# Heads' gated outputs go through device memory, and the first branch product becomes one stage over 16 row tiles behind the second branch's

## The chip, the cores and the metric

The kernel runs on one core of one Trainium2 chip. The metric is the device time of one launch in microseconds (us): lower is better. The kernel before takes 1253.05 us, the median of three runs (1251.77 to 1256.2).

## The reference

One layer of a hybrid decoder for a prompt group of 512 tokens and a sample group of 8 sequences of 4 tokens, 544 tokens in all, each of width 1024. Cut to what matters:

```
z = rmsnorm(h) @ W_in            # columns: q | k | v | gate | u | gv | gA | gB
q, k = rotary(q), rotary(k) / 16
o, s_new = retention(q, k, v, s0)        # 4 heads, decay per head; sample group starts from state s0
y_a = silu(gate) * rmsnorm_per_head(o)   # 4 heads x 512 = 2048 wide
gv  = layernorm(gelu(gv))
y_b = gelu(u) * spatial_gating(gv)       # 1024 wide
h += (sigmoid(gA) * (y_a @ W_br_a) + sigmoid(gB) * (y_b @ W_br_b)) @ W_o
h += relu(rmsnorm(h) @ W_up)**2 @ W_down # 4096 wide
h += sigmoid(rmsnorm(h) @ W_pg) * (p @ W_pp)
y = rmsnorm(h)
```

Outputs are y for both groups, the retention states of both groups, and the sample group's gv. All arithmetic counts as float32.

## The kernel before

Activations lie feature by token: a "slot" is a tile of 128 features by 544 tokens (`[P, T]`), and 56 slots, later 68 and 74, are handed out in turn by `get` and `put` (the slot freed longest ago comes first). A float32 operand is split into a high part (rounded, by a copy on ScalarE, line 127) and a low part (a subtraction on VectorE, line 128). TensorE takes three products for each: high times high, high times low, low times high.

A weight slab is 128 by 1024 values (512 KB). `Feed` loads slabs in the order in which they were planned (lines 535 to 573) into `raw` buffers, splits them ahead of use into "wide" buffers `hl`, and hands them to the products by `take`. There are four `hl` buffers (`ROOM1`), in the whole program. A "plain" product (`tile_of`, `dense`, line 315) makes one tile of 128 features: 8 steps over k, each of 3 products by 2 token halves of 272, so 48 matmuls. A "fast" run (`fast_run`, line 404) makes two tiles with 7 block products of 12 matmuls in place of 8, by sums of weight blocks and of activation blocks (Strassen's scheme with seven products). A pair takes three wide buffers, `w0`, `w1`, `w3`, and a small one. The copy on line 426 takes the first block product out of `fa` so that the next can add to it, and TensorE waits for that copy.

The stages in order:

- Four heads. Each makes two query and two key tiles, turns them (`rotary`, lines 685 to 690), makes four value tiles (`values`) and four gate tiles (`gates`). Around them stand the small steps of retention: transposes of the sample group's keys (`sample_keys`; GpSimd copies them out, line 787, TensorE transposes the copy, line 790), `scores` (line 849), the states' load, update and store (`state_ahead`, `sample_state`, 8 for each head, four buffers), `prompt_output`, and then `group_norm` and `group_normed`, which leave the head's four tiles of y_a as eight split slots `c.ya`.
- `branch_a(h, ya)`: for each of 8 output tiles, 4 steps over k, 24 matmuls. For heads 0 to 2 it is called in the next head, between its first pair of value tiles and the second. ScalarE copies each result from PSUM (line 711), and GpSimd issues an accumulating DMA to device memory, `acc_d` (line 712). For head 3 it stands alone behind the gv stage; there the eight sums are loaded again (line 702), and VectorE adds the products (line 715).
- gv: 4 fast pairs with transposes (`gated_by_token`); then branch_a for head 3, under which gv's layer norm is made; u: 4 fast pairs with `spatial`; gate A: 4 fast pairs, multiplied into the sums at once; gate B: 4 fast pairs, with the split of y_b (`gated`) beside them.
- y_b @ W_br_b tile by tile, with `merged` (lines 1216, 1217); W_o; the wide layer; the embedding gate; the last norm.

What sets the order: the small steps are put on a list with a due time (`chores`, `later`), and `tick` runs the due ones; a plain product ticks once every 12 matmuls, and a fast pair seven times. The due times are tables at the top (`QK`, `KEYS`, `SCORES`, `STATE`, `END`, `XOPS`). On top of that a scheduler places the instructions of each engine by its own estimate, and only pinned ones keep the program's order. Each engine then works strictly in that order.

Of the kernel before, what the change touches and what calls it, by code (L numbers as in the profile page):

```python
# [8 lines left out]
F32 = mybir.dt.float32  # L9
# [5 lines left out]
P = 128  # L15
# [8 lines left out]
H = 4  # L24
# [8 lines left out]
MORE = (12, 6)  # L33
ROOM1 = (4, 4, 1, 5)
ROOM2 = (1, 0, 0, 6)
# [3 lines left out]
STATES = 4  # L39
# [5 lines left out]
QK = ((7, 8, 9, 10), (0, 18, 2, 20))  # L45
KEYS = ((11, 16, 17), (22, 27, 28))
SCORES = (16, 24)
# [5 lines left out]
END = (17, 18, 22, 30)  # L53
# [37 lines left out]
def layer(tc, a, o):  # L91
    nc = tc.nc
    act, dve, pool, pe = nc.scalar, nc.vector, nc.gpsimd, nc.tensor
    with ExitStack() as ctx:
# [436 lines left out]
        def plan_branch_a(h):  # L531
            for m2 in range(4):
                feed.plan("plain", a["w_br_a"][4 * h + m2])

        for h in range(H):
            for p in range(6):
# [6 lines left out]
                if h and p == 2:  # L543
                    plan_branch_a(h - 1)
        for i in range(48, 56, 2):
            feed.plan("fast", a["w_in"][i], a["w_in"][i + 1])
        plan_branch_a(H - 1)
        for i in range(56, 80, 2):
            feed.plan("fast", a["w_in"][i], a["w_in"][i + 1])
        for n in ("w_br_b", "w_o"):  # L550
            for k in range(8):
                feed.plan("plain", a[n][k])
# [140 lines left out]
        acc_a = [None] * KD  # L693
        dp = enter(tc.tile_pool(name="sums", bufs=1, space=bass.MemoryType.DRAM))
        acc_d = [dp.tile([P, T], F32, tag=f"a{m}", name=f"acc{m}") for m in range(KD)]

        def branch_a(h, ya):

            if h == H - 1:
                for m in range(KD):  # L700
                    acc_a[m] = get()
                    nc.sync.dma_start(acc_a[m], acc_d[m])
            for m2 in range(4):
                w = feed.take()
                for i in range(2):
                    m = 2 * m2 + i
                    ps = Product()
                    dense(ps, [(*at(w, k * 256 + i * P), *ya[k]) for k in range(4)])
                    if h < H - 1:
                        t = get()  # L710
                        act.copy(halves(t), ps.all)
                        pool.dma_start(acc_d[m], t, accum_op=ALU.add if h else ALU.bypass)
# [3 lines left out]
            for y in ya:  # L716
                put(*y)
# [480 lines left out]
        for x in gvt:  # L1198
            put(*x)
# [372 lines left out]
```

## Time and profile before

| | |
|---|---|
| time, median of 3 runs (range) | 1253.05 us (1251.77 to 1256.2) |
| profiled execution, its own time | 1253.85 us |
| its span, first to last instruction | 1252.2 us |
| TensorE busy | 1226.6 us, 98% |
| VectorE, ScalarE, GpSimd busy | 900.4, 652.1, 101.9 us |
| granted TensorE clock, mean | 0.995 |
| DMA | 193.16 MB, mean 154 GB/s |

Line numbers are those of the kernel before. In a row of the chain or of the timeline, `f`, `fa`, `sc`, `ks` are PSUM tiles, `s` is any slot, `hl` a split weight slab, `acc` the sums in device memory, `x12` the number of instructions, and square brackets hold the idle time of the engine ahead of the row and what ended it. Matmul records can be missing, a few in a hundred, so a count of a little under the true number is no sign. The 1.65 us between the profiled execution's own time and its span lie around the program.

### The profile page before, as it was taken

What the parts mean: (1) busy time and instruction counts of PE and PEld (TensorE: products, weight loads), DVE (VectorE), ACT (ScalarE), POOL (GpSimd) and SP (SyncE); (2) the same over time, 40 slices, a digit from 0 to 9 for tenths busy, and PEclk for the clock granted to TensorE, in tenths of its full rate; (3) what the DMA queues carried; (4) which work ended last, traced back from release to release, by engine and by line L of the source; (5) the groups of instructions that cost most, each with busy time, mean ns of one, the idle gap of its engine ahead of it and who ended that gap; (6) DMA issues with size and microseconds to landing.
All of it is one profiled execution on the core that took longest, in us unless ns stands there. A gap on an engine that the chain in (4) does not pass through costs nothing.

```text
span 1252.2 us, 22976 instructions
## 1 busy us (share of the span) xinstructions
PE 1226.6 (98%) x9336; PEld 1196.7 (96%) x9336; DVE 900.4 (72%) x1341; ACT 652.1 (52%) x1106; POOL 101.9 (8%) x135
## 2 busy tenths in 40 slices
PE   8999999999999989999999999999999999999996
PEld 8998999999989988899999999999999999999996
DVE  6976957774767556678678645559449888878966
ACT  7553545444643555573466532436238558467733
POOL 0001111102010111111000000000000100000000
PEclk9999999999999999999999999999999999999999
DMA  8428544727664665675456462223346666766402
GB/s 284 168 93 272 168 157 134 245 100 168 170 223 133 164 157 175 220 203 142 119 138 178 146 211 94 85 85 99 105 101 179 175 178 160 182 165 180 140 1 72
DMA packets 73754, 193.16 MB, mean 154 GB/s; under 512 B 8400, under 2 KB 11728, under 8 KB 73648
## 3 DMA queue, kind: packets, MB, share of 16 engines
q1 hardware_dynamic: 58608, 141.42, 34.1%
q0 software_dynamic: 15040, 50.27, 18.0%
q8 instruction: 73, 1.20, 0.4%
q14 instruction: 33, 0.27, 0.1%
HBM read 163.74 MB, written 27.92 MB: 153 GB/s over the span
## 4 chain that ended last, share of the span: by engine, by line
PE 81%; DVE 5%; DMA 4%; issue 4%; ACT 3%; POOL 1%; SPq 0%; DVEq 0%; ACTq 0%; POOLq 0%
PE f L315 35%; PE fa L404 18%; PE f L404 14%; PE pg L315 4%; PE o L491 2%; PE st L491 2%; DMA acc<-s 1%; DVE hl L128 1%; PE so L914 1%; PE sc L491 1%; PE so L915 1%; ACT hl L127 1%; DVE s L128 1%; PE su L917 1%; DMA s<-in_xT 1%
## 5 line engine op out<-in xcount | busy, mean ns | idle before, releaser
L315 PE MATMUL f<-s,hl 128*128 128x272 f32 x4320 | 574.1, 290 | 3.4 <-ACT s L646 1.5
L315 PEld LDWEIGHTS f<-s,hl 128*128 128x128 f32 x4320 | 559.2, 189 | 11.5 <-ACT s L646 1.8
L128 DVE TENSOR_TENSOR hl<-raw,hl 128x1024 fp32r<-128x1024 f32 (+2 forms) x275 | 301.4, 1112 | 116.7 <-ACT hl L127 114.6
L127 ACT CAST hl<-raw 128x1024 fp32r<-128x1024 f32 (+2 forms) x275 | 259.9, 960 | 172.4 <-PE f L315 89.2
L404 PE MATMUL fa<-s,hl 128*128 128x272 f32 x2112 | 296.0, 289 | 3.9 <-ACT s L426 3.6
L404 PEld LDWEIGHTS fa<-s,hl 128*128 128x128 f32 x2112 | 276.0, 188 | 5.7 <-ACT s L426 4.6
L404 PE MATMUL f<-s,hl 128*128 128x272 f32 x1584 | 227.5, 290 | 1.4 <-ACT s L437 1.2
L404 PEld LDWEIGHTS f<-s,hl 128*128 128x128 f32 x1584 | 209.7, 189 | 2.8 <-ACT s L437 2.3
L127 ACT CAST s<-s 128x544 fp32r<-128x544 f32 (+4 forms) x170 | 97.4, 598 | 67.6 <-DMA acc<-s 15.5
L128 DVE TENSOR_TENSOR s<-s,s 128x544 fp32r<-128x544 f32 (+4 forms) x170 | 108.2, 658 | 16.1 <-DMA acc<-s 8.2
L127 ACT CAST s<-state 128x512 fp32r<-128x512 f32 x64 | 37.9, 620 | 51.6 <-DMA state<-in_state 34.7
L918 DVE SCALAR_TENSOR_TENSOR state<-state,su 128x512 f32<-128x512 f32 x64 | 42.5, 681 | 28.2 <-PE su L917 28.2
L128 DVE TENSOR_TENSOR s<-state,s 128x512 fp32r<-128x512 f32 x64 | 42.8, 685 | 19.6 <-ACT s L127 18.2
L204 POOL DMA_DIRECT2D raw<-in_w_in x20 | 17.7, 885 | 258.9 <-DMA raw<-in_w_in 68.2
L519 DVE RECIPROCAL s<-s 128x544 f32<-128x544 f32 (+1 forms) x9 | 28.6, 3173 | 10.6 <-ACT s L517 10.6
L204 POOL DMA_DIRECT2D raw<-in_w_up x12 | 10.2, 852 | 316.7 <-DVE s L128 180.3
L426 ACT COPY s<-fa 128x272 f32<-128x272 f32 x44 | 16.9, 384 | 33.3 <-PE fa L404 33.0
L451 DVE TENSOR_TENSOR s<-s,f 128x544 f32<-128x544 f32 x44 | 31.4, 714 | 3.4 <-PE f L404 3.4
L646 ACT COPY s<-f 128x544 f32<-128x544 f32 x24 | 14.6, 613 | 36.9 <-PE f L315 36.9
L315 PE MATMUL pg<-s,s 128*128 128x272 f32 x240 | 31.2, 289 | 0.1
L922 POOL DMA_DIRECT2D out_state_s<-state x32 | 23.3, 729 | 96.5 <-DVE state L918 96.4
L315 PEld LDWEIGHTS pg<-s,s 128*128 128x128 f32 x240 | 30.5, 188 | 0.4 <-DVE s L526 0.4
(174 smaller groups left out, 1156.8 us busy)
## 6 DMA issues: line engine op xcount, KB each, us to landing
raw<-in_w_in SPq DMA_DIRECT2D x58, 512.0 KB, 3.7
state<-in_state SPq DMA_DIRECT2D x32, 512.0 KB, 4.3
out_state_s<-state POOLq DMA_DIRECT2D x32, 512.0 KB, 4.2
raw<-in_w_in SPq DMA_DIRECT2D x60, 256.0 KB, 3.5
raw<-in_w_in POOLq DMA_DIRECT2D x20, 512.0 KB, 5.9
raw<-in_w_up SPq DMA_DIRECT2D x20, 512.0 KB, 3.3
raw<-in_w_down SPq DMA_DIRECT2D x20, 512.0 KB, 3.5
raw<-in_w_up SPq DMA_DIRECT2D x36, 256.0 KB, 3.4
```

Source lines behind the costliest of these rows:

```text
L127: act.copy(hi, src)
L128: dve.tensor_tensor(out=lo, in0=src, in1=hi.bitcast(F32), op=ALU.subtract)
L204: pool.dma_start(t, s1, accum_op=ALU.add)
L315: pe.matmul(ps.p[s], w, x[:, s * TH : (s + 1) * TH], start=first and i == 0 and j == 0, stop=last and i == n - 1 and j == 2, skip_group_ch ...
L404: pe.matmul(ps, a_, b_, start=first and k == j == 0, stop=k == 3 and j == 2, skip_group_check=True)
L426: act.copy(t0[:, lo_half], pa)
L451: dve.tensor_tensor(out=halves(x0), in0=halves(x0), in1=out.all, op=ALU.add)
L491: pe.matmul(ps[:rows, c], u, v, start=i == 0 and j == 0, stop=i == n - 1 and j == 2)
L519: dve.reciprocal(r[:, c], r[:, c])
L646: act.copy(halves(t), ps.all)
L918: dve.scalar_tensor_tensor(out=raw[:, i], in0=raw[:, i], scalar=gamma**LS, in1=ps, op0=ALU.mult, op1=ALU.add)
L922: pool.dma_start(o["state_s"][b, c.h].rearrange("(i p) v -> p i v", i=2), raw)
```

## The change

- `branch_a` goes, with its three-way traffic: no product, no copy and no accumulating DMA inside the heads. `group_normed` no longer splits: it multiplies, and GpSimd issues a plain DMA of the float32 tile to device memory (`ya_d`, 16 tiles).
- The order behind the heads is gv, gate A, u, gate B, then y_b @ W_br_b, whose tiles are multiplied with gate B, then y_a @ W_br_a as one stage: 8 output tiles, each over 16 row tiles in one PSUM accumulation. The 16 tiles of y_a are loaded and split during the stages just before (`head_tile`, `HEADS`).
- Value pairs of heads 2 and 3 are one fast run of two pairs; they were two runs of one.
- Room: six state buffers, were four; three wide weight buffers in the heads, were four, and five behind the first gv pair, were four; four slots fewer behind it. That hand-over stands after the first gv pair, was after the second.
- Due times are drawn in by the ticks that branch_a no longer gives: from the end of the key tiles on, `sample_keys` is due at tick 7, was 22; the scores at 11 to 14, were 24 to 27. Head 3's `group_norm` is due at 44, was 22. The loads of x for the fast operands are pinned.

The diff, cut to its core:

```diff
-MORE = (12, 6)
-ROOM1 = (4, 4, 1, 5)
-ROOM2 = (1, 0, 0, 6)
+MORE = (8, 6)
+ROOM1 = (4, 3, 1, 5)
+ROOM2 = (1, 2, 0, 6)
-STATES = 4
+STATES = 6
-KEYS = ((11, 16, 17), (22, 27, 28))
-SCORES = (16, 24)
+KEYS = ((11, 16, 17), (7, 9, 10))
+SCORES = (16, 11)
...
-                if h and p == 2:
-                    plan_branch_a(h - 1)
...
-                    n = next((i for i, p in enumerate(ps) if i and p == 3 or p not in FAST[h]), len(ps))
+                    n = next((i for i, p in enumerate(ps) if p not in FAST[h]), len(ps))
...
-        def branch_a(h, ya):
-
-            if h == H - 1:
-                for m in range(KD):
-                    acc_a[m] = get()
-                    nc.sync.dma_start(acc_a[m], acc_d[m])
-            for m2 in range(4):
-                w = feed.take()
-                for i in range(2):
-                    m = 2 * m2 + i
-                    ps = Product()
-                    dense(ps, [(*at(w, k * 256 + i * P), *ya[k]) for k in range(4)])
-                    if h < H - 1:
-                        t = get()
-                        act.copy(halves(t), ps.all)
-                        pool.dma_start(acc_d[m], t, accum_op=ALU.add if h else ALU.bypass)
-                        put(t)
-                    else:
-                        dve.tensor_tensor(out=halves(acc_a[m]), in0=halves(acc_a[m]), in1=ps.all, op=ALU.add)
...
             t = c.gate[m]
             dve.tensor_tensor(out=t, in0=t, in1=c.ro, op=ALU.mult)
-            hi, lo = get(F32R), get(F32R)
-            split(hi, lo, t)
-            c.ya.append((hi, lo))
+            pool.dma_start(ya_d[4 * c.h + m], t)
...
-                if m2 == 0 and before is not None:
-                    branch_a(before.h, before.ya)
...
-        branch_a(before.h, before.ya)
...
+        for t2 in fast_run([(x_ops, AF.Sigmoid)] * 4):
+            sig_a += t2
         for u2 in fast_run([(x_ops, AF.Gelu)] * 4):
...
+        def head_tile(k):
+            t = get()
+            nc.sync.dma_start(t, ya_d[k])
+            later(3, lambda: head_operand(k, t))
...
+        chores([(n, head_tile, k) for k, n in enumerate(HEADS)])
+        for m, ps in enumerate(tiles_from(yb)):
+            dve.tensor_tensor(out=halves(sig_b[m]), in0=ps.all, in1=halves(sig_b[m]), op=ALU.mult)
...
-            ps, t = tile_of(yb), get()
-            dve.tensor_tensor(out=halves(t), in0=ps.all, in1=halves(sig_b[m]), op=ALU.mult)
-            dve.tensor_tensor(out=t, in0=t, in1=acc_a[m], op=ALU.add)
+            ps, t = Product(), get()
+            for i in range(2):
+                w = feed.take()
+                xw = [(*at(w, k * P), *ya[8 * i + k]) for k in range(KD)]
+                dense(ps, xw, first=i == 0, last=i == 1)
+            dve.tensor_tensor(out=halves(t), in0=ps.all, in1=halves(sig_a[m]), op=ALU.mult)
+            dve.tensor_tensor(out=t, in0=t, in1=sig_b[m], op=ALU.add)
```

ScalarE's queue in head 3 before, between the last results of head 2's branch product and the second pair of value tiles (`f` and `fa` are PSUM, `hl` weight slabs, `km` and `k` the sample keys, `vh` values by token, `s` slots):

```order
L711 COPY s_402_4970<-f 128x544
L711 COPY s_407_5006<-f 128x544
L127 CAST hl<-raw 128x1024
L711 COPY s_412_5054<-f 128x544
L797 CAST k_5078<-s_413_5077 96x256
L897 ACTIVATE km<-k_5078,maskb 96x256 x2
L711 COPY s_414_5102<-f 128x544
L127 CAST hl<-raw 128x1024
L426 COPY s_415_5127<-fa 128x272
```

The same place of ScalarE's queue now (lines are the changed kernel's: 130 for 127, 429 for 426, 772 for 797):

```order
L964 COPY v_4346<-s_354_4195 128x96
L772 CAST k_4321<-s_366_4320 96x256
L130 CAST shl<-sf 96x32
L872 ACTIVATE km<-k_4321,maskb 96x256 x2
L964 COPY v_4348<-s_355_4212 128x96
L429 COPY s_367_4350<-fa 128x272
L130 CAST vh<-vt 128x4x128
L130 CAST hl<-raw 128x1024
```

The copies out of the branch product are gone, and the copy on which TensorE waits (426, now 429) has the keys' casts and their masks ahead of it in their place.

VectorE's queue in head 1 before, from the last instruction of the key rotation (690) to the one that takes the transposed sample keys (794); 728, 351 and 352 prepare x for the fast operands, 128 splits:

```order
L690 TENSOR_TENSOR s_147_1700<-s_147_1700,s_151_1717 128x544
L128 TENSOR_TENSOR s_153_1738<-s_125_1289,s_152_1737 128x544
L728 SCALAR_TENSOR_TENSOR s_178_2036<-s_178_2036,gcols,s_37_346 128x544
L128 TENSOR_TENSOR s_180_2040<-s_142_1634,s_179_2039 128x544
L351 TENSOR_TENSOR s_172_1965<-s_166_1894,s_165_1893 128x272
L352 SCALAR_TENSOR_TENSOR s_172_1965<-s_171_1964,s_166_1894 128x272
L128 TENSOR_TENSOR hl<-raw,hl 128x1024
L128 TENSOR_TENSOR s_175_2016<-s_171_1964,s_174_2015 128x544
L128 TENSOR_TENSOR s_182_2044<-s_147_1700,s_181_2043 128x544
L728 SCALAR_TENSOR_TENSOR s_177_2035<-s_177_2035,gcols,s_37_346 128x544
L794 TENSOR_SCALAR s_191_2132<-ks,sts 96x256
```

The same stretch now (688 for 690, 769 for 794, 703 for 728, 131 for 128):

```order
L688 TENSOR_TENSOR s_143_1697<-s_143_1697,s_145_1711 128x544
L131 TENSOR_TENSOR s_152_1789<-s_142_1637,s_151_1788 128x544
L131 TENSOR_TENSOR hl<-raw,hl 128x1024
L703 SCALAR_TENSOR_TENSOR s_146_1744<-s_146_1744,gcols,s_37_349 128x544
L131 TENSOR_TENSOR s_154_1793<-s_143_1697,s_153_1792 128x544
L703 SCALAR_TENSOR_TENSOR s_147_1745<-s_147_1745,gcols,s_37_349 128x544
L346 TENSOR_TENSOR s_159_1833<-s_146_1744 128x272
L769 TENSOR_SCALAR s_161_1856<-ks,sts 96x256
```

Nine instructions between the rotation and the transposed keys have become six, nearly all of them still with two inputs from SBUF.

GpSimd's queue in head 3 before, from the branch product to the first state stored:

```order
L712 DMA acc_216<-s_402_4970 128x544
L712 DMA acc_217<-s_407_5006 128x544
L204 DMA raw<-in_w_in 128x1024
L712 DMA acc_218<-s_412_5054 128x544
L712 DMA acc_219<-s_414_5102 128x544
L204 DMA raw<-in_w_in 128x1024
L882 DMA out_state_p<-s_443_5401 128x512
```

The same now (947 writes a tile of y_a of head 2, 762 is the sample keys' copy, 207 for 204):

```order
L947 DMA ya_220<-s_296_3331 128x544
L947 DMA ya_221<-s_312_3493 128x544
L947 DMA ya_222<-s_322_3612 128x544
L947 DMA ya_223<-s_333_3748 128x544
L762 COPY k_4314<-s_350_4097 128x96
L762 COPY k_4317<-s_351_4160 128x96
L207 DMA raw<-in_w_in 128x1024 x2
L857 DMA out_state_p<-s_395_4634 128x512
```

The eight accumulating writes behind the keys' copies have become four plain writes ahead of them.

More of the change, by code (lines that the diff above doesn't have):

```diff
@@ L52 @@
 PROMPT_OUTPUT = (9, 11, 16, 17)
-END = (17, 18, 22, 30)
+END = (17, 18)
+NORM = ((22, 30), (22, 30), (22, 30), (44, 46))
+GATED = 2
+HEADS = (0, 2, 4, 6, 8, 10, 12, 14, 16, 18, 20, 21, 22, 23, 24, 25)
 LAST = KD - 4
@@ L542, in layer @@
                         feed.plan("plain", w)
-                if h and p == 2:
-                    plan_branch_a(h - 1)
-        for i in range(48, 56, 2):
+        for i in (*range(48, 56, 2), *range(64, 72, 2), *range(56, 64, 2), *range(72, 80, 2)):
             feed.plan("fast", a["w_in"][i], a["w_in"][i + 1])
[L547 to L552, printed above, removed]
+        for k in range(8):
+            feed.plan("plain", a["w_br_b"][k])
+        for m in range(KD):
+            for i in range(2):
+                feed.plan("plain", a["w_br_a"][8 * i + m])
+        for k in range(8):
+            feed.plan("plain", a["w_o"][k])
         for n in ("w_up", "w_down"):
@@ L691, in rotary @@
             put(b, d)
-        acc_a = [None] * KD
-        dp = enter(tc.tile_pool(name="sums", bufs=1, space=bass.MemoryType.DRAM))
-        acc_d = [dp.tile([P, T], F32, tag=f"a{m}", name=f"acc{m}") for m in range(KD)]
-        def branch_a(h, ya):
-            if h == H - 1:
-                for m in range(KD):
-                    acc_a[m] = get()
-                    nc.sync.dma_start(acc_a[m], acc_d[m])
-            for m2 in range(4):
-                w = feed.take()
-                for i in range(2):
-                    m = 2 * m2 + i
-                    ps = Product()
-                    dense(ps, [(*at(w, k * 256 + i * P), *ya[k]) for k in range(4)])
-                    if h < H - 1:
-                        t = get()
-                        act.copy(halves(t), ps.all)
-                        pool.dma_start(acc_d[m], t, accum_op=ALU.add if h else ALU.bypass)
-                        put(t)
-                    else:
-                        dve.tensor_tensor(out=halves(acc_a[m]), in0=halves(acc_a[m]), in1=ps.all, op=ALU.add)
-            for y in ya:
-                put(*y)
+        dp = enter(tc.tile_pool(name="heads_out", bufs=1, space=bass.MemoryType.DRAM))
+        ya_d = [dp.tile([P, T], F32, tag=f"y{k}", name=f"ya{k}") for k in range(4 * H)]
         x_ops = []
@@ L1011, in gates @@
                     c.gate.append(t)
-        before = None
         for h in range(H):
@@ L1053, in layer @@
                 plan += [(AHEAD[b], state_ahead, c, b), (STATE[b], sample_state, c, b)]
-            chores(plan + [(END[3] + m, group_normed, c, m) for m in range(4)])
+            chores(plan + [(NORM[h][1] + m, group_normed, c, m) for m in range(4)])
             gates(c)
-            before = c
         gvt = [[None, None] for _ in range(5)]
@@ L1111, in layer @@
             chores([(2 * j + 1, gated_by_token, 2 * i + j, t) for j, t in enumerate(t2)])
-            if i == 1:
+            if i == 0:
                 head_pools.close()
@@ L1191, in layer @@
             chores([(1 + 3 * i, spatial, len(us) - 2 + i) for i in range(2)])
-        sig_b = []
-        for m, t2 in enumerate(fast_run([(x_ops, AF.Sigmoid)] * 4)):
-            for i in range(2):
-                dve.tensor_tensor(out=acc_a[2 * m + i], in0=acc_a[2 * m + i], in1=t2[i], op=ALU.mult)
-            put(*t2)
-        for x in gvt:
-            put(*x)
-        gp.close()
-        slots.grow(enter(tc.tile_pool(name="slots3", bufs=1, side="right")), MORE[1])
         def gated(m):
             yb[m] = operand(us[m])
-        chores([(1 + 3 * m, gated, m) for m in range(KD)])
-        for t2 in fast_run([(x_ops, AF.Sigmoid)] * 4):
+        for i, t2 in enumerate(fast_run([(x_ops, AF.Sigmoid)] * 4)):
             sig_b += t2
+            if i == 0:
+                for x in gvt:
+                    put(*x)
+                gp.close()
+                slots.grow(enter(tc.tile_pool(name="slots3", bufs=1, side="right")), MORE[1])
+                chores([(GATED * m, gated, m) for m in range(KD)])
         for x in xs:
```

25 lines of the change are left out of this document (14 added, 11 removed).

## Prediction

> **What bounds the kernel now.** I read the page first, then TensorE's waits, then windows of busy time, then the accumulating writes' tile and the timeline around each wait. From the page, the span and its first part (busy us, share, instructions):
>
> ```profile
> span 1252.2 us, 22976 instructions
> PE 1226.6 (98%) x9336; PEld 1196.7 (96%) x9336; DVE 900.4 (72%) x1341; ACT 652.1 (52%) x1106; POOL 101.9 (8%) x135
> ```
>
> TensorE is the bound: 25.6 us of 1252.2 are idle, and this change can only touch those, unless it makes more. The waits of TensorE (total us, times, longest), the rows that lie in or near the heads:
>
> ```profile
> PE fa L404 <- ACT s L426: 3.6, 4, 1.8
> PE sc L491 <- DVE s L849: 2.8, 1, 2.8
> PE ks L790 <- POOL k L787: 2.0, 1, 2.0
> ```
>
> Windows, each row a stretch, its length, busy us of TensorE, weight loads, VectorE, ScalarE, GpSimd with counts, then the granted clock, DMA share and GB/s. The first is inside head 0, the next three are heads 1, 2 and 3, the fifth lies in a dense stretch behind them, the last four follow two of the waits:
>
> ```profile
> 50.00:75.00 25.00, 25.00 (x199) 24.70 (x199) 23.15 (x38) 14.18 (x28) 2.09 (x3) 1.00 0.52 174
> 128.00:254.00 126.00, 123.95 (x892) 117.94 (x891) 91.74 (x144) 62.41 (x107) 18.22 (x23) 0.99 0.54 180
> 254.00:384.00 130.00, 127.81 (x933) 121.56 (x933) 85.28 (x128) 62.98 (x109) 18.62 (x24) 1.00 0.58 168
> 384.00:518.00 134.00, 130.69 (x943) 124.39 (x944) 86.58 (x129) 63.67 (x111) 17.89 (x24) 0.99 0.55 154
> 675.00:700.00 25.00, 25.00 (x202) 25.00 (x201) 18.21 (x23) 15.73 (x27) 1.70 (x2) 1.00 0.68 187
> 156.30:160.00 3.70, 3.70 (x21) 3.70 (x22) 3.70 (x7) 1.26 (x3) 0.61 (x1) 0.65 0.28 80
> 160.00:163.00 3.00, 3.00 (x24) 3.00 (x22) 1.29 (x2) 0.00 (x0) 0.00 (x0) 0.86 0.54 175
> 453.00:457.00 4.00, 4.00 (x21) 3.97 (x22) 2.72 (x5) 2.04 (x5) 0.00 (x0) 0.67 0.26 104
> 457.00:460.00 3.00, 3.00 (x24) 3.00 (x23) 1.41 (x2) 1.14 (x2) 0.00 (x0) 0.87 0.00 0
> ```
>
> A matmul takes 25.00/202 = 0.124 us where nothing waits. The clock column shows a second cost: behind two waits it is granted only in part. At 156.3 to 163 that loses 3.70 x 0.35 + 3.00 x 0.14 = 1.7 us, at 453 to 460 it loses 4.00 x 0.33 + 3.00 x 0.13 = 1.7 us.
>
> Now each wait. TensorE's timeline (start, us, row, idle before and what ended it):
>
> ```profile
> 156.26 0.31 PE L790 MATMUL ks<-ident,k 128*96 128x128 f32 x1 [1.96 <-POOL k L787]
> ...
> 301.16 1.02 PE L315 MATMUL f<-s,hl 128*128 128x272 f32 x6 [1.07 <-ACT s L711]
> ...
> 319.37 1.79 PE L404 MATMUL fa<-s,hl 128*128 128x272 f32 x12 [1.11 <-ACT s L426]
> ...
> 448.19 1.77 PE L404 MATMUL fa<-s,hl 128*128 128x272 f32 x12 [0.52 <-ACT s L426]
> ...
> 452.87 1.32 PE L491 MATMUL sc<-s,s 128*128 128x384 f32 x6 [2.78 <-DVE s L849]
> ...
> 532.14 0.52 PE L404 MATMUL fa<-s,hl 128*128 128x272 f32 x2 [1.79 <-ACT s L426]
> ```
>
> The second to fifth stand in the branch product of heads 2 and 3 or just behind it. The tile of the sums in device memory says why; who waited for its writes to land, us and times:
>
> ```profile
> who waited for it (us, times):
>   ACT s L127: 15.5, 4
>   DVE s L128: 8.2, 4
>   DVE s L794: 7.3, 2
>   DVE s L849: 3.0, 1
> ```
>
> Slots that the copies of line 711 filled come round again while their write is still under way, and ScalarE and VectorE stop in order behind that. VectorE's timeline ties the largest wait to it:
>
> ```profile
> 452.12 0.69 DVE L849 TENSOR_TENSOR s<-sc,dtab 128x512 f32<-128x512 f32 x1 [3.01 <-DMA acc<-s]
> ```
>
> **The change, part by part.** The groups of instructions that it moves (count, busy us, mean ns, idle before):
>
> ```profile
> L128 DVE TENSOR_TENSOR hl<-raw,hl 128x1024 fp32r<-128x1024 f32 (+2 forms) x275 | 301.4, 1112 | 116.7 <-ACT hl L127 114.6 <-DMA raw<-in_w_br_b 1.2
> L127 ACT CAST hl<-raw 128x1024 fp32r<-128x1024 f32 (+2 forms) x275 | 259.9, 960 | 172.4 <-PE f L315 89.2 <-issue 26.8 <-PE f L404 25.9
> L128 DVE TENSOR_TENSOR s<-s,s 128x544 fp32r<-128x544 f32 (+4 forms) x170 | 108.2, 658 | 16.1 <-DMA acc<-s 8.2 <-ACT s L127 7.8
> L127 ACT CAST s<-s 128x544 fp32r<-128x544 f32 (+4 forms) x170 | 97.4, 598 | 67.6 <-DMA acc<-s 15.5 <-DVE s L849 10.3 <-DVE s L344 6.0
> L712 POOL DMA_DIRECT2D acc<-s x24 | 18.2, 777 | 68.5 <-ACT s L711 55.4 <-ACT v L994 12.6 <-issue 0.4
> L711 ACT COPY s<-f 128x544 f32<-128x544 f32 x24 | 14.4, 612 | 16.3 <-PE f L315 13.8 <-DMA acc<-s 2.5
> L715 DVE TENSOR_TENSOR s<-s,f 128x544 f32<-128x544 f32 x8 | 5.6, 705 | 3.0 <-PE f L315 2.9
> ```
>
> TensorE's own work stays: 4 heads x 8 tiles x 24 = 768 matmuls before, 8 tiles x 96 = 768 now, 95 us by 0.124, in another place. Off the path go ScalarE's 24 copies (14.4 us), VectorE's eight adds (5.6 us) and 24 accumulating DMAs on GpSimd (18.2 us, less 16 plain issues); neither engine is the bound, so their busy time is worth nothing by itself. What counts is the waits.
>
> Gone with the branch product: 1.07 (its own PSUM copy), 1.11 and 0.52 (the copy of line 426 late behind it), 2.78 (the scores) and the clock's 1.7 behind that. Sum 7.2 us. The y_a writes in their place are four in a head, issued in the next head's query and key tiles, where no scores wait; I charge them nothing, and one wait of the 0.52 us kind if a slot comes round too early.
>
> The wait of 1.96 us at 156.26 is head 1's sample keys: GpSimd's copy of them is late. Its row (min/median/max ns), and what VectorE did meanwhile:
>
> ```profile
> L787 POOL COPY k<-s x8: 263/516/4282, 57.1 to 415.6; 128x96 f32<-128x96 f32 x8
> ```
> ```profile
> 151.69 1.22 DVE L128 TENSOR_TENSOR hl<-raw,hl 128x1024 fp32r<-128x1024 f32 x1
> 152.82 1.99 DVE L128 TENSOR_TENSOR s<-s,s 128x544 fp32r<-128x544 f32 x3
> 154.73 0.71 DVE L690 TENSOR_TENSOR s<-s,s 128x544 f32<-128x544 f32 x1
> ```
>
> A copy of 263 ns took up to 4282 ns while VectorE ran two-input operations back to back. In head 1 the rotation now stands ahead of the work for the fast operands in VectorE's order, so this one wait should go, with its clock: 1.96 + 1.7 = 3.7 us. But the keys are now due 7 ticks behind the key tiles in heads 1 to 3, 10.4 us by 12 x 0.124 a tick, where heads 2 and 3 had 22. VectorE needs six operations of 0.71, 4.3 us, for a key's rotation and has six more queued before it stops for the transposed keys (the order above); those are the ones that starve the copy. Bounds for each head: 0 (the copy at 263 ns) and 1.96; I take the middle, 0.98, three times: 2.9 us. [...]
>
> The wide buffers: with three instead of four, the next fast pair's first slab goes into what the first slab of the running pair frees. Between the two stand 24 matmuls, 3.0 us, and the split takes 0.96 + 1.11 = 2.07. The slack of 0.9 us holds if both engines are free. If not, the nearest row is the 1.11 us wait at 319.37. Between 0 and 1.11 I take 0.5 at each of three boundaries (heads 2 and 3, first gv pair): 1.5 us. A gain below zero is excluded: fewer buffers allow nothing earlier.
>
> The wait of 1.79 at 532.14 lies behind two table loads for head 3's group norm:
>
> ```profile
> 526.40 1.28 ACT L517 ACT_TABLE_LOAD   x1
> ...
> 528.20 1.28 ACT L449 ACT_TABLE_LOAD   x1
> ```
>
> That norm is moved out of gv to the start of gate A, and the layer norm's square root, which had the branch product as cover, falls into gate A too. The loads move with it, so I count the 1.79 as kept, between 0 and twice that.
>
> The new stage: per output tile TensorE has 96 x 0.124 = 11.9 us; ScalarE needs 2 x 0.96 + 0.60 = 2.5 us, VectorE 2 x 1.11 + 0.66 + 2 x 0.7 = 4.3 us. In the y_b stage, 47.5 us of TensorE, VectorE has 8 x (0.7 + 1.11) + 16 x 0.66 = 25 us. Both are covered twice over. Six state buffers and the two more wide buffers behind the heads I count at nothing: no TensorE wait in the table is on a state, and late fast runs wait for ScalarE, not for a buffer.
>
> Sum: -7.2 - 3.7 + 2.9 + 1.5 = -6.5 us. Against the profiled execution's 1253.85 (span 1252.2, 1.65 around it) that is 1247.4; it ran 0.8 above the median of 1253.05, so I put the time at 1246.6, and the rivals below are set against 1253.05 in the same way.
>
> [...]
>
> **The rivals.**
>
> - All that is listed goes and nothing new comes: -7.2 - 3.7 - 1.8 = -12.7, so 1240.4 by the median. For it: head 0 has no branch product, its VectorE is at 23.15 of 25, and TensorE is busy all of those 25 us. Against it: three buffers and the earlier keys.
> - Starved copies: GpSimd's copy of the sample keys is late in each of heads 1, 2 and 3 by the full 1.96 with the clock's 1.7, 11.0 us for the 2.9: -7.2 - 3.7 + 11.0 + 1.5 = +1.6, so 1254.7, no change. For it: the 4282 ns row; against it: VectorE itself stops for the transposed keys after six operations and then leaves the copy alone.
> - Pauses cost only their own length: the two 1.7 fall out of the gain, -6.5 + 3.4 = -3.1, 1250.0, no change. Against it are the two rows of 0.65 and 0.67. [...]
> - Slower: VectorE becomes the bound in the heads. Per head 192 matmuls, 23.8 us of TensorE, go, but of VectorE only 4 x 1.11 + 4 x 0.66 = 7.1 us. Head 1 then needs 84.6 of 102.2 us (83%), head 2 78.2 of 106.2 (74%), head 3 79.5 of 110.2 (72%). Between key rotation and scores it is denser than that, since 16 ticks in which it stood idle are gone. It decides where that stretch asks for more than its length: then TensorE pauses at the keys and again at the scores, six pauses of 1.96 + 1.7 = 22 us: -10.9 + 22 + 1.5 = +12.6, so 1265.7. Against it: head 0's 93% without a wait.
>
> **How the numbers follow.** A measurement of this kernel can tell about 0.3%, 3.8 us, from no change: faster is below 1249.3, slower above 1256.8. My forecast has 0.55, its own range 1242.2 to 1251.4 (-10.9, with the keys between 0 and 5.9 and the buffers between 0 and 3.3), with 0.05 of it above 1249.3. All gone: 0.08. Starved copies: 0.22, spread about 1254.7, of which 0.02 is below 1249.3 and 0.04 above 1256.8. Pauses at their own length: 0.04, no change. VectorE bound: 0.11. Faster 0.50 + 0.08 + 0.02 = 0.60, same 0.05 + 0.16 + 0.04 = 0.25, slower 0.04 + 0.11 = 0.15. The range 1240.5 to 1255.5 leaves out the 0.11, some 0.06 of the starved copies and little below.
>
> **What would show it.** Right: TensorE idle near 19 us, no wait on `L849` in head 3, no clock row below 1.00 at the scores, ScalarE and VectorE without any wait on writes of y_a. The keys' step: a wait `ks <- POOL` of 1 us or less in each of heads 1 to 3, and none as long as 1.96. The buffers' step: short waits at the second pair of heads 2 and 3, ended by a cast or a subtraction into `hl`. Wrong: three long `ks` waits with half clock behind them, VectorE above 90% in heads 1 to 3 with TensorE waiting for it, or waits of `f` on the split of y_a in the new stage.

## The result and the profile after

The changed kernel takes 1238.8 us, the median of four runs (1238.44 to 1238.86); the kernel before took 1252.41 us beside it (four runs, 1251.02 to 1256.2). The ratio is 0.9886, its 95% interval 0.9864 to 0.9908. The gain is 13.6 us (11.5 to 17 by the interval), twice the forecast of 6.5, and the time lies 1.7 us below the forecast range. The rival "all that is listed goes and nothing new comes", 1240.4 at a chance of 0.08, came nearest.

The profiled execution took 1238.44 us. From its page the span and the engines:

```profile
span 1236.8 us, 23016 instructions
PE 1220.6 (99%) x9336; PEld 1192.5 (96%) x9336; DVE 895.9 (72%) x1333; ACT 636.6 (51%) x1082; POOL 92.4 (7%) x127
```

The span is 15.4 us shorter. Busy time of VectorE and ScalarE fell by 4.5 and 15.5 us, which by itself is worth nothing, as they were no bound. TensorE's idle time went from 25.6 to 16.2 us, and its busy time fell by 6.0 us although it does the same 9336 matmuls. So 9.4 us came out of pauses, and 6.0 out of matmuls that no longer run long.

Of TensorE's waits (total us, times, longest), three of before that the prediction did not quote:

```profile
PE f L315 <- ACT s L646: 1.5, 1, 1.5
PE f L404 <- ACT s L437: 1.2, 2, 0.7
...
PE so L914 <- ACT s L127: 0.5, 1, 0.5
```

and the longest that are left:

```profile
PE norm L518 <- DVE s L1416: 1.6, 1, 1.6
...
PE f L318 <- ACT s L528: 1.0, 1, 1.0
PE norm L518 <- ACT s L461: 0.9, 1, 0.9
PE f L407 <- DVE hl L131: 0.5, 1, 0.5
PE fa L407 <- ACT s L429: 0.5, 1, 0.5
```

What counts is what is missing: there is no row of `ks` or `sc`, and none longer than 1.6 us. Nor does any of these rows lie in a head: the longest is in the last norm, that for line 528 is ahead of the first product, that for line 461 is at 476 us, right behind gv, and the two of 0.5 stand in the wide layer, behind 1040 us. All rows of this view add up to 6.6 us; those of before added up to 16.1. The difference of 9.5 is the 9.4 of the page.

Windows over the second half of head 0 and over heads 1, 2 and 3 (columns as in the prediction):

```profile
50.00:126.00 76.00, 76.00 (x529) 70.47 (x528) 60.55 (x101) 37.76 (x70) 11.34 (x14) 1.00 0.63 212
126.00:229.00 103.00, 103.00 (x739) 97.23 (x738) 84.46 (x138) 52.97 (x93) 13.44 (x20) 1.00 0.60 199
229.00:332.00 103.00, 102.85 (x736) 97.00 (x735) 77.86 (x118) 51.97 (x92) 13.74 (x20) 1.00 0.58 186
332.00:436.00 104.00, 103.85 (x745) 98.06 (x744) 80.04 (x122) 53.91 (x97) 13.54 (x19) 1.00 0.49 151
```

TensorE has no pause worth the name in 386 us. VectorE is at 82, 76 and 77% of heads 1 to 3, where the prediction worked out 83, 74 and 72: denser in heads 2 and 3, and still no bound. The clock column is 1.00 throughout, so both half-clock stretches (in the kernel before the granted clock was 0.50 from 158.3 to 160.3 and from 455 to 457 us), 3.4 us together, are gone as forecast.

The writes of y_a in the changed kernel, by the median from issue to landing, and who waited for the tile:

```profile
ya<-s POOLq DMA_DIRECT2D x16, 272.0 KB, 3.2
...
  ACT s L130: 6.5, 3
```

The writes of the sums in the kernel before, in the same view: first those of head 0, then of head 1, then of head 2 (each made in the next head).

```profile
acc<-s POOLq DMA_DIRECT2D x8, 272.0 KB, 2.5
...
acc<-s POOLq DMA_DIRECT2D x8, 272.0 KB, 5.9
...
acc<-s POOLq DMA_DIRECT2D x8, 272.0 KB, 6.1
```

Of the 24 writes that the prediction calls accumulating, 16 are. Those of head 0 begin the sums and are plain (`ALU.bypass` in the diff): they landed after 2.5 us in the median, and nobody waited for them. The accumulating ones took 5.9 and 6.1 us, and engines waited 36.5 us in all behind them (15.5, 8.2, 7.3 and 3.0 in the tile's rows in the prediction, and 2.5 at the end of line 711's). A median of 5.8 us for the accumulating writes and of 3.7 for those of y_a, as one expectation below has them, mixes in the loads of the same tiles. The 6.5 us of ScalarE's waits that remain are at 614 to 629 us, for the loads of y_a ahead of the new stage, and no wait of TensorE follows from them.

### The profile page after: what moved, and what is told of

Read it like the earlier page. It is cut to its first block, busy times and chain, and to the rows that moved or that the text cites. A ratio compares the mean times of both kernels' runs of the same rounds, so it can differ in the third digit from the quotient of the medians.

```text
span 1236.8 us, 23016 instructions
## 1 busy us (share of the span) xinstructions
PE 1220.6 (99%) x9336; PEld 1192.5 (96%) x9336; DVE 895.9 (72%) x1333; ACT 636.6 (51%) x1082; POOL 92.4 (7%) x127
## 3 DMA queue, kind: packets, MB, share of 16 engines
q0 software_dynamic: 13376, 48.04, 16.3%
## 4 chain that ended last, share of the span: by engine, by line
PE 92%; DVE 4%; ACT 2%; DMA 1%; issue 1%; SPq 0%; DVEq 0%; ACTq 0%
PE f L318 41%; PE fa L407 20%; PE f L407 15%; PE o L494 2%; PE pg L318 2%; PE st L494 2%; PE sc L494 1%; PE su L892 1%; PE so L889 1%; PE so L890 1%; DVE s L522 1%; DVE hl L131 1%; ACT hl L130 1%; PE sp L1124 1%; PE vt L835 1%
## 5 line engine op out<-in xcount | busy, mean ns | idle before, releaser
L318 PE MATMUL f<-s,hl 128*128 128x272 f32 x4320 | 567.2, 289 | 1.2 <-ACT s L528 1.0
L407 PE MATMUL fa<-s,hl 128*128 128x272 f32 x2112 | 291.7, 289 | 1.1 <-ACT s L429 0.5
L407 PE MATMUL f<-s,hl 128*128 128x272 f32 x1584 | 225.0, 289 | 0.7 <-DVE hl L131 0.5
L130 ACT CAST s<-s 128x544 fp32r<-128x544 f32 (+3 forms) x170 | 97.9, 596 | 28.0 <-DMA s<-ya 6.5
L131 DVE TENSOR_TENSOR s<-s,s 128x544 fp32r<-128x544 f32 (+3 forms) x170 | 107.2, 657 | 4.2 <-ACT s L130 2.8
L255 DVE TENSOR_TENSOR raw<-raw 128x512 f32<-128x512 f32 x44 | 30.4, 694 | 0.6
L254 DVE TENSOR_TENSOR raw<-raw 128x512 f32<-128x512 f32 x44 | 30.5, 695 | 0.4
```

Of the source, the lines that this page charges most:

```text
L130: act.copy(hi, src)
L131: dve.tensor_tensor(out=lo, in0=src, in1=hi.bitcast(F32), op=ALU.subtract)
L254: dve.tensor_tensor(out=t[:, 512:], in0=t[:, 512:], in1=v[:, :512], op=ALU.add)
L255: dve.tensor_tensor(out=t[:, :512], in0=t[:, 512:], in1=v[:, 512:], op=ALU.add)
L318: pe.matmul(ps.p[s], w, x[:, s * TH : (s + 1) * TH], start=first and i == 0 and j == 0, stop=last and i == n - 1 and j == 2, skip_group_ch ...
L407: pe.matmul(ps, a_, b_, start=first and k == j == 0, stop=k == 3 and j == 2, skip_group_check=True)
```

## The experiments

Each kernel is compared with runs of the kernel before on the same chip, which it shares with three others. A letter says which: beside (a) the median of the kernel before was 1254.89 us, beside (b) 1254.83, beside (c) 1253.65. A control in (b), the changed kernel with an empty line in it, shows what repeats:

> The changed kernel once more with no edit but an empty line, as the control for the three beside it: 0.989 of the kernel before, as measured.

It took 1238.58 us (1238.41 to 1238.89), 0.9868 of the kernel before (0.985 to 0.9887). The changed kernel's runs lie within 0.5 us; the 13 runs of the kernel before beside it went from 1251.9 to 1258.8, so the gain is 16.3 us against these.

### The accumulating writes

**Left out (a).** The kernel before, with the writes of heads 1 and 2 gone. The copies out of PSUM stay, and so does everything else:

```diff
-                        pool.dma_start(acc_d[m], t, accum_op=ALU.add if h else ALU.bypass)
+                        if h == 0:
+                            pool.dma_start(acc_d[m], t)
```

> The kernel before, with the accumulating writes of heads 1 and 2 left out (their products are computed and copied out of PSUM, and then dropped, so y_a's branch lacks two heads). Theory W, slots whose write has not landed stop ScalarE and VectorE: the waits of 1.07, 1.11, 0.52 and 2.78 us in heads 2 and 3 and the half clock behind the scores (1.7) go, 7.2 us, to 1245 (1243.5 to 1247); the wait on the sample keys in head 1 stays, since no write stands before it. Rival D, the due times and the place of the product do it, the writes are only what the waits are named after: 1251 or more, with waits of the same length ended by something else.

It took 1242.7 us (1242.05 to 1244.63), 0.9907 (0.9887 to 0.9928): 12.2 us gained by the medians, 9.0 to 14.2 by the interval. Two rows of TensorE's timeline of this run, the transposed keys of head 1 and the fast pair in gv that the prediction showed at 156.26 and 532.14:

```profile
154.53 0.31 PE L791 MATMUL ks<-ident,k 128*96 128x128 f32 x1 [1.75 <-POOL k L788]
...
520.54 0.52 PE L404 MATMUL fa<-s,hl 128*128 128x272 f32 x2 [1.79 <-ACT s L426]
```

Both waits are still there, so they are not from the writes, but between the two rows lie 366.0 us, where there were 375.9. Of the 9.9 us, 1.7 is the half clock that stood behind the keys' wait and does not stand there in this run; no write lies ahead of that wait, so it is not the writes' doing. The other 8.2 us are the writes' price in this stretch of the profiled runs: the prediction's four waits and the half clock behind the largest make 7.2 of it, and 1.0 has no row of its own. The theory holds, and the size was a little low.

**Plain in place of accumulating (c).** The kernel before once more and the same queue, with a plain write of the same 272 KB at each place, so that the sums over the heads are left out:

```diff
-                        pool.dma_start(acc_d[m], t, accum_op=ALU.add if h else ALU.bypass)
+                        pool.dma_start(acc_d[m], t)
```

> The kernel before with plain writes in place of the accumulating ones, at the same places of the same queue; the sums over the heads are left out. If what stalls the engines is that an accumulating write takes longer to land (median 5.8 us, against 3.7 of the plain writes of the changed kernel), the landing falls to some 4 us and the time comes near that of the run without the writes: 1243 to 1247. If any write from the round of slots in this dense stretch lands late enough, whatever its kind, the time stays: 1250 to 1254, with landings of 5 us or more.

It took 1244.66 us (1240.86 to 1246.03), 0.9926 (0.9907 to 0.9945), a gain of 9.0 us. Who waited for the tile of the sums in this run, and the landing of the writes of heads 1 and 2:

```profile
  ACT s L127: 1.9, 2
  DVE s L849: 1.8, 1
  DVE s L128: 1.5, 2
  DVE s L794: 1.1, 2
...
acc<-s POOLq DMA_DIRECT2D x8, 272.0 KB, 2.8
...
acc<-s POOLq DMA_DIRECT2D x8, 272.0 KB, 2.6
```

The waits fell from 36.5 to 6.3 us, the landing from 5.9 and 6.1 to 2.8 and 2.6 us, and none of what is left reaches TensorE in the branch product. Its timeline has the two rows of above at

```profile
154.07 0.31 PE L790 MATMUL ks<-ident,k 128*96 128x128 f32 x1 [1.75 <-POOL k L787]
...
520.07 0.52 PE L404 MATMUL fa<-s,hl 128*128 128x272 f32 x2 [1.79 <-ACT s L426]
```

366.0 us apart, as without any write in heads 1 and 2. So the price came neither from writing the products out nor from the place of the writes, but from their accumulating: in this stretch of the profiled runs that alone is worth all that leaving the writes out is. By the medians of the whole kernel it is 9.0 of 12.2, with intervals that overlap.

### The keys

**The copy made four times (b).** The changed kernel, with GpSimd's copy of the sample keys repeated. Four times the work on the suspected engine; the scheduler then also places the second key's transpose 1.1 to 1.9 us behind the first in heads 1 to 3, where the two stood together:

```diff
-                pool.tensor_copy(
-                    r.rearrange("p (a s) -> p a s", a=3), t[:, None, LP:].to_broadcast([P, 3, NS])
-                )
+                for _ in range(4):
+                    pool.tensor_copy(
+                        r.rearrange("p (a s) -> p a s", a=3), t[:, None, LP:].to_broadcast([P, 3, NS])
+                    )
```

> The changed kernel with GpSimd's copy of the sample keys made four times over, to see how much room the keys' step has. In the profile of the changed kernel the copies of heads 1 to 3 take 0.6 to 1.2 us each and end 4 us ahead of the transposes. My prediction's term (the copy is late by about 1 us as it is): three more copies for each of two keys in each of three heads come on top in full, 3 us or more a head with half clock behind, 10 us or more above the control. Theory W with room of 4 us: 0 to 4 us above the control.

It took 1244.93 us (1243.94 to 1246.18), 0.9919 (0.99 to 0.9939): 6.4 us above the control. First the changed kernel's row of the copies (min/median/max ns), with one copy each:

```profile
L762 POOL COPY k<-s x8: 262/720/3017, 57.3 to 354.6; 128x96 f32<-128x96 f32 x8
```

Then TensorE's wait for keys with four, and the windows around it:

```profile
66.83 0.45 PE L766 MATMUL ks<-ident,k 128*96 128x128 f32 x1 [3.45 <-POOL k L763]
```
```profile
62.00:66.00 4.00, 1.38 (x12) 1.12 (x10) 4.00 (x8) 2.85 (x5) 4.00 (x1) 1.00 1.01 356
66.00:70.00 4.00, 3.17 (x16) 3.18 (x17) 1.00 (x2) 0.65 (x2) 2.44 (x7) 0.57 0.25 88
```

It is the only such wait, and it is in head 0, whose due times the change left alone: 3.45 us and 4.00 x 0.43 = 1.7 us of clock are 5.2 of the 6.4. In the stretch from 62 to 66, VectorE is busy for all 4.00 us, and GpSimd spends all 4.00 in a single copy. In heads 1, 2 and 3 the eight copies of a head keep GpSimd busy for 2.75, 5.07 and 5.07 us and still end ahead of the transposes. In the changed kernel itself they end 4.6, 2.9 and 2.9 us ahead of the transposes (the expectation had 4 for all). So the price that I put on the keys there, 0.98 us a head, was 0, with room for nearly three copies more. The 6.4 us lie between what the two theories of the expectation allowed: neither looked at head 0.

### The buffers

**Three wide buffers in the kernel before (a).**

```diff
-MORE = (12, 6)
-ROOM1 = (4, 4, 1, 5)
-ROOM2 = (1, 0, 0, 6)
+MORE = (8, 6)
+ROOM1 = (4, 3, 1, 5)
+ROOM2 = (1, 1, 0, 6)
```

> The kernel before with three wide weight buffers in the heads instead of four, four again behind them (the fourth stands where four slots stood). My prediction's term: up to 1.11 us at each boundary of fast pairs, so 1252.4 plus 0 to 3.3. Theory S, a fourth buffer lets ScalarE cast two slabs ahead of the first query copy and that is the 1.5 us wait at 21.4 us: that wait goes, 1251 or a little less. If neither, 1252.4 within 0.5.

It took 1263.43 us (1260.66 to 1264.68), 1.0067 (1.0045 to 1.0089): 8.5 us slower. Waits of TensorE that the kernel before did not have, or had shorter:

```profile
PE ks L790 <- POOL k L787: 5.6, 3, 3.1
PE fa L404 <- DVE hl L128: 2.8, 2, 2.4
PE f L404 <- ACT s L437: 2.4, 5, 0.5
```

Both readings of the expectation missed. 2.8 us are waits for the split itself, where the prediction charged 1.5: 0.46 in head 3, and 2.35 at 537 us in gv, behind four table loads. The rest are keys and copies that come late. With one buffer less VectorE's order is another, and three heads wait for the late copy (up to 4279 ns in this run) in place of one.

**Products in three tiles of their own (a),** on top of that, so that no slot stands behind an accumulating write:

```diff
-                        t = get()
+                        t = hp.tile([P, T], F32, tag="prod", name="prod", bufs=3)
...
-                        put(t)
```

> The kernel before with three wide buffers in the heads, as its control, and the branch products of heads 0 to 2 copied into three tiles of their own instead of into slots, so that no other work comes round to a tile whose write is under way; all work is done. Theory W: the waits of others on the writes go (15.5, 8.2, 7.3 and 3.0 us of ScalarE and VectorE to about 0), and the copy itself may wait for the landing three products back (9 us for a median landing of 4.5), so nearly all of the 7.2 us: 5 to 7 us below its control. Rival D: within 1 us of its control.

It took 1272.22 us (1271.95 to 1273.57), 1.0142 (1.0122 to 1.0163), slower still by 8.8. TensorE's longest wait:

```profile
PE ks L789 <- POOL k L786: 11.9, 3, 5.1
```

GpSimd's copies in this run:

```profile
L786 POOL COPY k<-s x8: 262/1888/7951, 55.9 to 423.3; 128x96 f32<-128x96 f32 x8
```

No engine waits for a write's landing in this run, but the keys' wait is 11.9 us. The run was to show the slots' part alone, and it cannot: in its control the writes reach TensorE with 0.4 us at most (a wait for line 426 in head 3; no row of `sc`, none of line 711), although ScalarE and VectorE wait 25.1 us for them. Why the keys come later still is open. A VectorE that is freed from its stalls behind the writes is hardly the reason: the copies start at 148.67, 283.25 and 418.53 us, ahead of the branch product of each head, whose first writes are at 166.6, 300.1 and 434.1. The run does show the rival of the starved copies at full size, in another kernel than the one it was written for.

**Four wide and four state buffers in the changed kernel (a), four state buffers alone (c).**

```diff
-ROOM1 = (4, 3, 1, 5)
-ROOM2 = (1, 2, 0, 6)
+ROOM1 = (4, 4, 1, 5)
+ROOM2 = (1, 1, 0, 6)
...
-STATES = 6
+STATES = 4
```

> The changed kernel with four wide buffers and four state buffers in the heads, as before the change; five wide buffers behind, slots as they are. Theory S: the wait at the start comes back, +1.5 us, and the short waits on a cast into the wide buffers in heads 2 and 3 go: 1239.5 (1238.5 to 1241). Rival B, the six state buffers carry part of the gain: TensorE or ScalarE waits for states again, over 1242.

> The changed kernel with four state buffers instead of six, nothing else. If the state buffers are worth nothing, as I counted them and as the run with four wide and four state buffers leaves them, the time is that of the changed kernel, 1238.2 to 1239.2, with the same waits of TensorE (0.5 and 0.2 into the wide buffers, 1.0 at 476). If they carry the keys (a key waiting for a state buffer would come too late for its copy), there is a wait of ks or sc in heads 1 to 3 and 1241 or more.

With both: 1237.17 us (1236.01 to 1240.81), 0.987 (0.9846 to 0.9893). With four state buffers alone: 1238.78 us (1238.17 to 1239.2), 0.9884 (0.9869 to 0.9898). The states are worth nothing, as counted. The wide buffer is worth 1.4 us against the control by the medians and nothing by the ratios (0.987 and 0.9868), so no gain is shown. Of the expectation the wait at the start came back; the short waits in heads 2 and 3 that it wanted gone were hardly there (0.2 us in the control, in head 2). What the buffer moves is seen at the start of the program. TensorE's wait there, first in the run with four wide buffers:

```profile
21.66 5.76 PE L318 MATMUL f<-s,hl 128*128 128x272 f32 x44 [1.64 <-ACT s L644]
```

then ScalarE's timeline of the same run:

```profile
19.13 1.97 ACT L130 CAST hl<-raw 128x1024 fp32r<-128x1024 f32 x2
21.01 1.11 ACT L644 COPY s<-f 128x544 f32<-128x544 f32 x2
```

and ScalarE's in the changed kernel, with three:

```profile
17.97 1.04 ACT L130 CAST hl<-raw 128x1024 fp32r<-128x1024 f32 x1
18.91 0.59 ACT L644 COPY s<-f 128x544 f32<-128x544 f32 x1
19.41 1.05 ACT L130 CAST hl<-raw 128x1024 fp32r<-128x1024 f32 x1
```

With a fourth buffer free, ScalarE casts two slabs in a row, and the first query tile's copy comes behind them; TensorE waits for the PSUM tile that the copy frees. With three, there is no room for the second cast until a slab has been used, the copy goes first, and TensorE does not wait. The size varies: this wait is 0.8 to 2.1 us in the six profiled runs with four buffers, and 0 to 0.5 in those with three. The kernel before had this wait too, 1.5 us in its table of waits, from the copy on line 646; the prediction did not list it. So fewer buffers did allow something earlier, which the prediction excluded.

### Head 3's group norm

**Due at 22 again (b), the same with four wide buffers (c), and later, at 48 (c).** The last two have four wide and four state buffers; the last has (48, 50) in the place of (44, 46):

```diff
-NORM = ((22, 30), (22, 30), (22, 30), (44, 46))
+NORM = ((22, 30), (22, 30), (22, 30), (22, 30))
```

> The changed kernel with head 3's group norm due at 22 ticks as in the other heads, so that its square root falls into gv again as before the change. Theory W holds the wait of 1.79 us behind the table loads to be the norm's place: it comes back in gv (1.5 to 2 us, perhaps with half clock, 1.7) and the wait of 0.95 at the start of gate A goes: 1 to 3 us above the control. Rival D, the place does not matter: within 0.5 us of the control.

> The changed kernel with four wide and four state buffers in the heads, five behind them, and head 3's group norm due at 22 again. If the norm at 22 costs its 8 us by the table loads alone, this is 8 above the 1237.2 of the run with four wide buffers: 1244 to 1247. If it costs that only because three wide buffers leave the fast pair no cover behind the loads (the wait into hl of 2.5 us at 454), the fourth buffer covers it: 1238 to 1241, and no wait into hl near 454.

> The changed kernel with four wide and four state buffers in the heads, five behind them, and head 3's group norm due at 48 instead of 44. The 1.0 us that TensorE waits at the layer norm's sums near 476 stands behind table loads of that group norm; if the loads are the cause, moving them on by four ticks takes it away: 1235.8 to 1237. If the wait is one of the order of the layer norm itself, it stays: 1236.5 to 1237.8.

At 22 with three wide buffers: 1246.73 us (1245.53 to 1247.92), 0.9933 (0.9913 to 0.9953), 8.1 above the control. At 22 with four: 1240.82 (1239.98 to 1240.98), 0.9899 (0.9884 to 0.9914), 3.7 above the kernel with four. At 48 with four: 1241.12 (1239.84 to 1245.63), 0.9899 (0.9883 to 0.9916), 3.9 above; both of these ranges overlap that of the kernel with four. The first result is far above what either reading foresaw, the second is as its second reading had it, the third is above both. The first and the last of ScalarE's four table loads with the norm at 22 and three buffers, then VectorE's timeline behind them:

```profile
438.00 1.28 ACT L520 ACT_TABLE_LOAD   x1
...
444.51 1.28 ACT L452 ACT_TABLE_LOAD   x1
```
```profile
444.53 3.56 DVE L522 RECIPROCAL s<-s 128x544 f32<-128x544 f32 x1 [0.58 <-ACT s L520]
...
449.74 2.62 DVE L946 TENSOR_TENSOR s<-s,s 128x544 f32<-128x544 f32 x4
...
452.88 3.48 DVE L131 TENSOR_TENSOR hl<-raw,hl 128x1024 fp32r<-128x1024 f32 x3
```

and TensorE's wait and the window behind it:

```profile
454.15 2.55 PE L407 MATMUL fa<-s,hl 128*128 128x272 f32 x10 [2.48 <-DVE hl L131]
```
```profile
454.20:457.80 3.60, 3.60 (x17) 3.60 (x18) 2.17 (x2) 0.39 (x1) 0.00 (x0) 0.53 0.88 270
```

Four loads of 1.28, 5.1 us within 8, then VectorE's reciprocal and products, 6.2 us, push the splits back, and the fast pair waits for them: 2.48 and 1.7 us of clock are 4.2 of the 8.1, and the rest lies in smaller waits from 441 to 510. With four wide buffers the wait into `hl` at 454 is gone, two of 1.28 and 1.16 at 444 to 448 stand behind the loads, and 3.7 remain. So with three buffers the norm's new place is worth 8.1 us, and more than half of that makes up for the missing buffer. At 48 a wait of 1.54 us into `hl` stands at 517.68, in gate A. But the profiled run there is the longest of the four, and it has half clock at 20 to 28 and at 220 to 228 us, 1.7 us each, far from the norm (its mean clock is 0.993, that of the other three 0.996), so what 48 costs is not settled.

The 0.95 us that TensorE waits in the changed kernel at 476 I had put down to the loads. With the norm at 48, ScalarE loads no table from 447 to 488, and the same wait still stands there, now before a fast pair:

```profile
482.08 1.76 PE L407 MATMUL fa<-s,hl 128*128 128x272 f32 x12 [0.95 <-ACT s L461]
```

so it belongs to the copy out of PSUM on line 461 and not to the loads. In this the second reading of that expectation was right, though not in the time.

### The due times

**Head 0's due times in all heads (b),** with four state buffers, and 59 slots for 56 to hold what then lives longer:

```diff
...
-QK = ((7, 8, 9, 10), (0, 4, 2, 6))
-KEYS = ((11, 16, 17), (7, 9, 10))
-SCORES = (16, 11)
+QK = ((7, 8, 9, 10), (7, 8, 9, 10))
+KEYS = ((11, 16, 17), (11, 16, 17))
+SCORES = (16, 16)
```

> The changed kernel with later due times in heads 1 to 3, those of head 0: key rotation at 7, queries at 10, sample keys at 11, scores at 16 to 19 (they were 0, 6, 7 and 11 to 14); four state buffers and 59 slots, then 64 as before, since it holds more slots. Theory W: due times alone move nothing by over 2 us, since nothing in the heads waits for a write. Rival D, the drawn-in times carry the gain: VectorE and ScalarE crowd in the gates' part, TensorE waits there, 4 us or more above the control.

It took 1247.03 us (1242.29 to 1253.22, ten runs), 0.9941 (0.9922 to 0.9961). The two longest waits:

```profile
PE so L889 <- ACT s L130: 2.3, 1, 2.3
PE gt L1039 <- ACT s L466: 1.9, 2, 1.5
```

The first, at 115.49, is in head 0, whose due times are the same in both kernels, and with the half clock behind it (1.7 us; the next matmul begins 0.43 us after one of 512 columns there, and 0.23 us ahead of the wait) it is 4.0 of the 8.4; most likely the slots have a part in it. No key waits, early or late, and no wait in heads 1 to 3 is over 0.7 us, so the time is that of rival D and its mechanism is not seen. What the earlier due times are worth by themselves stays open. So does what the value pairs in one run and the pinned loads of x are worth: no run has either alone.

## Why the prediction was wrong

The direction was right and so was the mechanism behind the largest term; the size was half of what came. The step that failed is the charge for what the change adds, the earlier keys (+2.9) and the third buffer (+1.5): both measured 0 in the heads. By its steps:

- **What bounds the kernel,** TensorE's pauses and the half clock behind some of them: right. The 15.4 us of the span are 9.5 of named waits, 3.4 of clock, and 2.5 that no row of the waits shows.
- **The writes, 7.2:** right in kind, a little low in size. 8.2 us between head 1's keys and gv in the profiled runs; 9.0 to 14.2 over the whole kernel by the interval of the run without the writes. What the prediction did not see is why they landed late: plain writes at the same places cost TensorE nothing there, and those of head 0, which are plain, never did.
- **Head 1's keys, 3.7:** right. The wait and its clock are gone. The 1.7 of clock in it is not sure to come, though: in the run without the writes the same wait, at 1.75 us, has none behind it.
- **The earlier keys, +2.9: this is the step that failed most.** I took "the middle" between 0 and 1.96 in three heads because a copy had once taken 4282 ns. What came is 0: no `ks` wait in any head. The copies did stretch, to 3017 ns in head 0, but nothing waited, and in heads 1 to 3 the two of a head took 1.5 to 1.8 us together. I had priced the copy and not the time from its end to the transpose that needs it, 2.9 to 4.6 us; the run with four copies shows that four of them nearly fit there. What stretches a copy is not shown, and that VectorE starves it was my reading: in the kernel before VectorE runs without a gap beside the copy of 4282 ns (busy 4.28 of 4.28 us from 151.93) and beside one of 0.27 us at 60.72 as well.
- **Three wide buffers, +1.5:** failed as well: 0 at the three boundaries that I charged, 0.2 us in the control. The 0.5 us into `hl` in the changed kernel's table stands in the wide layer, where it has five wide buffers:

```profile
1047.69 0.89 PE L407 MATMUL f<-s,hl 128*128 128x272 f32 x5 [0.53 <-DVE hl L131]
```

  Against the charge, 1.5 us went at the start, by the same third buffer, where the prediction had excluded a gain. That the price was small is owed to the norm's place: with it at 22, one buffer is worth 5.9 us by the medians (1246.73 against 1240.82), and in the kernel before, with its norm at 22, one buffer less brought a wait of 2.35 us behind the table loads.
- **The 1.79 us in gv, kept:** it went, and the norm's place is why: with the norm at 22 waits come back there, of 2.48, 0.79 and 0.70 us. A wait of 0.95 came at 476, of another cause.
- **New stage, states, writes of y_a, 0 each:** right. TensorE waits for no split of y_a.
- **The clock.** The pauses of 1.96 and 2.78 us had half clock behind them, and the forecast counted it; the 3.4 us came. But not every pause has it. The run with plain writes has one of 1.75 us, whose row stands above at 154.07, and one of 1.79 at 520.07. Windows around both:

```profile
152.00:156.00 4.00, 2.25 (x19) 2.03 (x18) 4.00 (x8) 2.82 (x5) 2.72 (x2) 1.00 0.55 178
156.00:160.00 4.00, 4.00 (x34) 4.00 (x33) 3.60 (x6) 0.65 (x2) 0.00 (x0) 1.00 0.45 145
...
520.00:524.00 4.00, 3.79 (x20) 3.54 (x21) 4.00 (x6) 2.52 (x14) 0.73 (x1) 0.70 0.41 148
524.00:528.00 4.00, 4.00 (x30) 3.98 (x30) 3.98 (x6) 3.65 (x7) 0.17 (x1) 0.88 0.82 133
```

  The first pause keeps its clock at 1.00, the second loses 4.00 x 0.30 + 4.00 x 0.12 = 1.7 us. In the kernel before the pause at the same instruction, 1.79 us at 532.14, kept its clock too (1.00 from 528 to 540). So the length of a pause does not tell by itself: of two of 1.79 us one cost clock and one did not. What decides it, these runs do not show. Where the windows in this document and in the prediction have it below 1.00, the loss is 1.7 us each time.

Together, in us of the profiled runs, the span fell by 8.9 more than the forecast's 6.5. The two charges that did not come make 4.4. Waits that went beside those that I had listed make 3.8: 1.8 in gv, 1.5 at the start, 0.5 in head 0. New waits take back 1.4: 0.9 at 476 and 0.5 ahead of the first product. Behind 900 us, in stages whose work the change leaves alone, waits add up to 3.1 before and 3.5 now, which takes back 0.4. The 2.5 without a row make up the sum and stay open: matmuls that ran a little long with no wait that the profile names. By the medians the gain is 1.8 less than by the profiled runs, since that of the kernel before was 1.4 above its median here, and that of the changed kernel 0.4 below.

The rival whose time came nearest had it that nothing new comes. Its part on the keys and the buffers is what the runs showed; that its sum is so near is in part luck, since the new waits, and waits and long matmuls that it did not list, nearly cancel by the medians.

The forecast also spent 0.22 on the starved copies and 0.11 on VectorE as the bound. Neither was near, in this kernel; but two of the experiments above, with one buffer less in the kernel before, fell into the first.

No version tried is faster than the changed kernel by more than the runs can tell; the one with four wide buffers is 1.4 us lower in the median, with an overlapping range.

## What to carry to other kernels

When an in-order engine stops for a buffer, ask how long the transfer out of that buffer takes to land and not only how much it moves: here accumulating writes in the round of buffers held ScalarE and VectorE for 36.5 us and TensorE behind them for some 8, and plain writes at the same places held them for 6.3 and TensorE not at all. But only what reaches the bound counts: with one buffer less, 25.1 us of such waits reached TensorE with 0.4. Price a moved step by the slack between its end and its first reader, in rows, before charging it a share of the worst stall ever seen on its engine. A buffer count is also an order: one buffer less can hold an engine back from work that it would do too soon, as at the start of this program.

## What the runs showed of the hardware

In the kernel before, accumulating DMAs of a 128 by 544 float32 tile from GpSimd's queue landed 5.9 and 6.1 us after their issue in the median (heads 1 and 2), plain ones at the same places 2.8 and 2.6 us; in the run with tiles of their own all transfers of the sums, the plain writes of head 0 and the loads among them, landed after 4.5 us in the median, against 5.8 in the kernel before. A GpSimd copy of 128 by 96 values takes 0.26 us at its shortest; one took over 4.00 us while VectorE ran without a gap, one 0.27 us while it did so too, and the longest 7.95. Two pauses of TensorE of 1.75 and 1.79 us in one run cost nothing beside their length in the one case and 1.7 us in the other.
